# Gate and up products of two SwiGLUs by Strassen's scheme, down products as a second stage

## The chip, the cores and the metric

The kernel runs on one core of one Trainium2 chip. Its time is the device time of one execution in microseconds (us), the median of several runs. The core's engines run unsynchronized, each through its own queue in order: TensorE (PE in the profile, its weight loads PEld) multiplies matrices, VectorE (DVE) and ScalarE (ACT) do element-wise work and can read PE's accumulation banks in PSUM, GpSimd (POOL) does element-wise work on SBUF alone, and SyncE (SP) issues nearly all DMA transfers here. An instruction that waits holds up all that stands behind it on its engine.

## What is computed

One layer on x of 1024 tokens by 1024 features, float32, in three steps with a final norm. The token mixing between the two SwiGLUs is the same before and after.

```python
def rms_norm(x, g):
    y = x * lax.rsqrt(jnp.mean(x * x, axis=-1, keepdims=True) + NORM_EPS)
    return y * g
def swiglu(x, w_gate, w_up, w_down):       # w_gate, w_up: 1024 x 2816, w_down: 2816 x 1024
    return (jax.nn.silu(x @ w_gate) * (x @ w_up)) @ w_down

x = x + 0.5 * swiglu(rms_norm(x, ffn1_norm), ffn1_w_gate, ffn1_w_up, ffn1_w_down)
x = x + token_mixing(rms_norm(x, mix_norm))   # attention, mLSTM, output product
x = x + 0.5 * swiglu(rms_norm(x, ffn2_norm), ffn2_w_gate, ffn2_w_up, ffn2_w_down)
return rms_norm(x, final_norm)
```

## The kernel before

Everything lies transposed: features on the 128 partitions, tokens along the free axis, in two halves of 512 tokens (`HALVES`). A float32 product is made of three matmuls: each operand is split into a high part (ScalarE copies it to float32r) and a low part (the operand minus its high part, on VectorE), and `mm3` (L337) adds high x high, high x low and low x high in one PSUM bank. One matmul has 128 x 128 weights and 512 tokens.

`Weights` (L44) streams all weights of the program in one fixed order through three rings: a raw unit of 128 x 1024 (`wraw`, two buffers, loaded by SP), its high part (`whi`, four buffers, L71) and its low part (`wlo`, four, L83). A `get` splits the unit two places ahead, and loading runs ahead of splitting, over the borders between the stages of the program as well.

The order of all instructions is the program's own (`manual_schedule`). Side work is written as generators that stand in a list `bg`; `pump` (L264) lets each of them issue one more piece between two products, and `drain` issues the rest.

A SwiGLU is the function `ffn` (L343). The 22 blocks of 128 hidden features are taken in four groups of 6, 6, 5 and 5 (`GROUPS`). For each block, gate (w = 0) and up (w = 1) are multiplied for both halves of the tokens, 8 blocks of input features by 3 matmuls each; `evac` (L348) turns two such banks into a gated row, high and low part, in SBUF: a multiply by 1/rms (L351), tanh on ScalarE (L352), and so on to L358. After each group `down` (L414) multiplies its gated rows by the down weights for the 8 blocks of output features and adds the result to the rows of x in SBUF (L427). In the last group the first half goes through all output blocks ahead of the second, so that the next norm (`norm`, L312, with `rstd_of`, L280, for 1/rms) can begin.

The products start on rows that aren't normed yet: `gained` (L306) multiplies by the norm's gain and splits (L309, L310), and 1/rms of each token is applied to the product in `evac`. The first SwiGLU starts with `W.start`, which loads its first units in halves; `SHIFT` times `WARM` = 12 small matmuls on a constant matrix run while the first loads are on their way (L467). The second SwiGLU starts behind the output product of the second half (L1200 on), whose loop also prepares its rows; its first weight units are loaded and split meanwhile.

`late_consts` (L203) makes constants for the mixing within the first SwiGLU.

## Time and profile before

| | |
|---|---|
| median of 3 runs | 2546.78 us (2544.69 to 2547.41) |
| span of the profiled execution | 2542.7 us |
| PE busy | 2500.0 us, 98% |
| VectorE, ScalarE, GpSimd busy | 1268.5, 771.4, 251.5 us |
| DMA | 182 MB, 72 GB/s on average |

The profiled execution is one run of the program; its span reaches from the first to the last instruction. Busy times are sums over the span, and stages differ: GpSimd's, for instance, lie in the token mixing almost alone. An engine's idle time costs something only where another engine waits for it.

### The profile page before, as it was taken

How to read it: one execution, taken by the hardware profiler on the slowest of the kernel's cores; microseconds unless marked ns; L12 is line 12 of the kernel's file. 1: busy time of each engine (PE TensorE's matmuls, PEld its weight loads, DVE VectorE, ACT ScalarE, POOL GpSimd, SP SyncE). 2: the span in 40 equal slices, each digit the busy share in tenths (PEclk: the TensorE clock that was granted, in tenths of full speed). 3: DMA queues.
4: the chain of work that ended last, by engine and by line, in shares of the span. 5: the costliest groups of instructions: out<-in, count | busy, mean ns of one | idle time of the engine just before them, and what ended most of it. 6: DMA issues, size and time to landing. Idle time of an engine off the chain costs nothing.

```text
span 2542.7 us, 29518 instructions
## 1 busy us (share of the span) xinstructions
PE 2500.0 (98%) x11856; PEld 2077.6 (82%) x11856; DVE 1268.5 (50%) x2188; ACT 771.4 (30%) x1438; POOL 251.5 (10%) x218
## 2 busy tenths in 40 slices
PE   9999999999998999999999999999999999999997
PEld 7888888888887878888877788888888888888886
DVE  6533433434458873555658944545553343343444
ACT  5211111112236642333346623333321121111123
POOL 0000000000034330000234400000000000000003
PEclk9999999999999999999999999999999999999999
DMA  3111111121242212222532122224211111111113
GB/s 133 53 50 50 46 46 58 38 62 43 77 142 65 71 61 85 77 84 85 179 96 63 53 83 86 69 86 150 83 40 44 59 48 44 55 39 56 50 40 118
DMA packets 64841, 182.08 MB, mean 72 GB/s; under 512 B 7488, under 2 KB 12736, under 8 KB 64704
## 3 DMA queue, kind: packets, MB, share of 16 engines
q1 hardware_dynamic: 62640, 179.20, 22.4%
q8 instruction: 93, 1.52, 0.3%
q0 software_dynamic: 1200, 0.79, 0.2%
q14 instruction: 44, 0.36, 0.0%
q10 hardware_dynamic: 864, 0.21, 0.0%
HBM read 168.90 MB, written 11.27 MB: 71 GB/s over the span
## 4 chain that ended last, share of the span: by engine, by line
PE 86%; DVE 9%; ACT 2%; issue 1%; DMA 1%; SPq 0%; DVEq 0%; POOL 0%; ACTq 0%
PE mm L338 26%; PE mm L339 26%; PE mm L340 26%; DVE P L811 1%; PE mm L672 1%; DVE PT L850 1%; PE mm L673 1%; PE mm L674 1%; DVE P L831 1%; DVE wlo L83 1%; PE lm L952 1%; PE lm L980 1%; PE lm L975 1%; PE lm L978 1%; DVE s L621 0%
## 5 line engine op out<-in xcount | busy, mean ns | idle before, releaser
L338 PE MATMUL mm<-s,whi 128*128 128x512 f32 (+1 forms) x2992 | 1174.5, 393 | 1.9 <-ACT s L309 0.9
L340 PE MATMUL mm<-s,wlo 128*128 128x512 f32 (+1 forms) x2992 | 1165.4, 389 | 2.8 <-POOL wlo L83 2.8
L339 PE MATMUL mm<-s,whi 128*128 128x512 f32 (+1 forms) x2992 | 1164.6, 389 | 0.9 <-DVE s L310 0.9
L340 PEld LDWEIGHTS mm<-s,wlo 128*128 128x128 f32 x2992 | 563.5, 188 | 122.3 <-POOL wlo L83 4.9
L338 PEld LDWEIGHTS mm<-s,whi 128*128 128x128 f32 x2992 | 563.5, 188 | 118.5 <-issue 4.1
L339 PEld LDWEIGHTS mm<-s,whi 128*128 128x128 f32 x2992 | 564.1, 189 | 113.4 <-DVE s L310 2.2
L71 ACT ACTIVATE whi<-wraw 128x1024 fp32r<-128x1024 f32 (+3 forms) x320 | 310.8, 977 | 359.0 <-PE mm L339 269.3
L83 DVE TENSOR_TENSOR wlo<-wraw,whi 128x1024 fp32r<-128x1024 f32 (+2 forms) x290 | 333.6, 1151 | 100.0 <-ACT whi L71 99.0
L427 DVE SCALAR_TENSOR_TENSOR X<-mm,X 128x512 f32<-128x512 f32 (+1 forms) x132 | 88.5, 675 | 274.5 <-PE mm L340 274.4
L352 ACT ACTIVATE mm<-nsq 128x512 f32<-128x512 f32 x88 | 53.0, 602 | 380.3 <-DVE nsq L351 380.3
L351 DVE TENSOR_TENSOR nsq<-mm,nr 128x512 f32<-128x512 f32 x88 | 60.8, 691 | 213.8 <-PE mm L340 188.4
L355 DVE TENSOR_TENSOR nsq<-nsq,mm 128x512 f32<-128x512 f32 x88 | 60.4, 687 | 176.3 <-PE mm L340 176.1
L83 POOL TENSOR_TENSOR wlo<-wraw,whi 128x1024 fp32r<-128x1024 f32 (+1 forms) x30 | 61.2, 2043 | 702.9 <-ACT whi L71 701.3
L357 ACT ACTIVATE s<-nsq 128x512 fp32r<-128x512 f32 x64 | 40.5, 632 | 272.2 <-DVE nsq L356 268.4
L288 POOL TENSOR_TENSOR nv<-nv,mhalf 128x4 f32<-128x4 f32 (+1 forms) x9 | 11.2, 1242 | 911.4 <-DVE nv L287 911.4
L353 DVE SCALAR_TENSOR_TENSOR nsq<-mm,nsq 128x512 f32<-128x512 f32 x88 | 60.9, 692 | 58.9 <-ACT mm L352 58.9
L340 PE MATMUL mm<-gb,wlo 128*128 128x512 f32 (+1 forms) x196 | 75.5, 385 | 0.0
L339 PE MATMUL mm<-gb,whi 128*128 128x512 f32 (+1 forms) x196 | 75.5, 385 | 0.0
L338 PE MATMUL mm<-gb,whi 128*128 128x512 f32 (+1 forms) x196 | 75.5, 385 | 0.0
L672 PE MATMUL mm<-whi,s 128*128 128x256 f32 x256 | 74.1, 289 | 0.0
L673 PE MATMUL mm<-whi,s 128*128 128x256 f32 x256 | 72.5, 283 | 0.0
L674 PE MATMUL mm<-wlo,s 128*128 128x256 f32 x256 | 72.4, 283 | 0.0
(229 smaller groups left out, 2161.0 us busy)
## 6 DMA issues: line engine op xcount, KB each, us to landing
wraw<-gu SPq DMA_DIRECT2D x86, 512.0 KB, 3.7
wraw<-win SPq DMA_DIRECT2D x84, 512.0 KB, 3.5
wraw<-dn SPq DMA_DIRECT2D x48, 320.0 KB, 2.9
wraw<-dn SPq DMA_DIRECT2D x32, 384.0 KB, 3.1
wraw<-wmv SPq DMA_DIRECT2D x16, 512.0 KB, 3.2
wraw<-wpa SPq DMA_DIRECT2D x16, 512.0 KB, 3.2
wraw<-wpm SPq DMA_DIRECT2D x16, 512.0 KB, 3.2
wraw<-wwo SPq DMA_DIRECT2D x16, 512.0 KB, 3.3
```

Source lines behind the costliest of these rows:

```text
L71: self.nc.scalar.activation(hv, v, AF.Copy)
L83: (self.nc.gpsimd if self.on_pool else self.nc.vector).tensor_sub(lv, v, hv.bitcast(F32))
L338: nc.tensor.matmul(ps, hi, xh, start=first, stop=False)
L339: nc.tensor.matmul(ps, hi, xl, start=False, stop=False)
L340: nc.tensor.matmul(ps, lo, xh, start=False, stop=last)
L351: nc.vector.tensor_mul(t, ps, R[h])
L353: nc.vector.scalar_tensor_tensor(t, ps, 1.0, t, op0=OP.add, op1=OP.mult)
L355: nc.vector.tensor_mul(t, t, ps)
L427: nc.vector.scalar_tensor_tensor(x, ps[p], 0.25, x, op0=OP.mult, op1=OP.add)
L672: nc.tensor.matmul(ps, x[:, 0], hi, start=k == 0, stop=False)
L673: nc.tensor.matmul(ps, x[:, 1], hi, start=False, stop=False)
L674: nc.tensor.matmul(ps, x[:, 0], lo, start=False, stop=k == KT - 1)
```

## The change

Gate and up products are computed by the Winograd form of Strassen's scheme. The matrix of weights is cut into 2 x 2 blocks (two blocks of hidden features by two halves of the input features), the rows of x into 2 x 2 blocks as well (two halves of the features by two halves of the tokens); seven products of sums of blocks take the place of eight products. Since sums of x blocks mix tokens, the rows must be normed before: x times gain times 1/rms.

- `mixed` makes the sums of x blocks on GpSimd and splits them into high and low parts. Products 1 and 2 need only the first half of the tokens and no sums. They are done for two pairs of hidden blocks (s = 0 and 1) at the start, while `lead` norms the other half and runs `mixed`.
- `gate_up` goes through 11 pairs s of hidden blocks, with products in the order 1, 2, 6, 7, 4, 5, 3. Weight sums are made on GpSimd (`sums`, `last_sum`). A product's weights are split four products ahead (`split`, the same rings of four buffers). Products 1 and 2, then 6, 7 and 4, then 5 and 3 accumulate in one bank each; what is added from other banks is added by VectorE (`group`).
- `gated` writes the gated rows to a DRAM buffer `gd`. The down products follow as a second stage, in chunks of 2, 4, 4, 4, 4 and 4 hidden blocks: `fetch` loads a chunk's rows and splits them while the chunk before is multiplied; x is loaded again for the residual.
- Temporary rows of 128 x 512 share one ring of 24 buffers (`RING`).
- The second SwiGLU's weights don't belong to the stream of `Weights` any longer (`W.limit`); its first loads are issued when the output product is through. Its first half of rows is normed within the output product (`early`), with sums of squares on GpSimd.
- `W.start` is gone; the warm-up has 48 matmuls (`SHIFT` 12). `late_consts` runs at the end of `lead`. Final rows are stored one by one instead of in pairs.

```diff
-GROUPS = (6, 6, 5, 5)
+CHUNK = 4
+CHUNKS = [(0, FT % CHUNK)] + [(f, CHUNK) for f in range(FT % CHUNK, FT, CHUNK)]
+RING = 24
+PRODUCTS = (1, 2, 6, 7, 4, 5, 3)
-SHIFT = 3
+SHIFT = 12
...
+    def parted(x, hi, lo):
+        nc.scalar.activation(hi, x, AF.Copy)
+        nc.vector.tensor_sub(lo, x, hi.bitcast(F32))
+
+    def mixed(pool, Xn, op, own):
+        for k in range(4):
+            own[k] = [temp(pool, R32) for _ in range(2)]
+            t = temp(pool)
+            nc.gpsimd.tensor_sub(t, Xn[4 + k][1], Xn[k][1])
+            parted(Xn[4 + k][1], *own[k])
+            nc.gpsimd.tensor_sub(Xn[k][1], Xn[k][1], Xn[k][0])
+            nc.gpsimd.tensor_add(Xn[k][0], Xn[k][0], t)
+            nc.gpsimd.tensor_sub(Xn[4 + k][0], Xn[4 + k][0], Xn[k][0])
+            parted(Xn[k][0], op[6](k, 0), op[6](k, 1))
+            yield
+            parted(t, op[7](k, 0), op[7](k, 1))
+            parted(Xn[4 + k][0], op[4](k, 0), op[4](k, 1))
+            parted(Xn[k][1], op[5](k, 0), op[5](k, 1))
+            yield
...
+        def split(s, p):
+            if s == S2:
+                return
+            src = raw[s, *{1: (0, 0), 2: (0, 1), 6: "S2", 7: (0, 0), 4: (1, 1), 5: (1, 0), 3: (0, 1)}[p]]
+            hi = wpool.tile([128, UNIT], R32, name="whi", bufs=4)
+            lo = wpool.tile([128, UNIT], R32, name="wlo", bufs=4)
+            parted(src, hi, lo)
...
+        def sums(s):
+            if s < S2:
+                a11, a21, a22 = raw[s, 0, 0], raw[s, 1, 0], raw[s, 1, 1]
+                raw[s, "S", "2"] = t = pool.tile([128, UNIT], F32, name="wr", bufs=4)
+                nc.gpsimd.tensor_sub(a11, a11, a21)
+                nc.gpsimd.tensor_sub(t, a22, a11)
+                nc.gpsimd.tensor_add(a21, a21, a22)
+
+        def last_sum(s):
+            if s < S2:
+                nc.gpsimd.tensor_sub(raw[s, 0, 1], raw[s, 0, 1], raw[s, "S", "2"])
...
+        def gated(s, m, half, z, w, src):
+            if w == 0:
+                st["th"] = temp(pool)
+                nc.scalar.activation(st["th"], z[0], AF.Tanh, scale=0.5)
+            else:
+                th = st.pop("th")
+                nc.vector.scalar_tensor_tensor(th, th, 1.0, z[0], op0=OP.add, op1=OP.mult)
+                nc.vector.tensor_mul(th, th, z[1])
+                nc.sync.dma_start(gd[2 * s + m, :, half * HS:(half + 1) * HS], th)
+
+        def group(s, p):
+            for w in range(2):
+                ps = product(s, p, w, p in (1, 6, 5))
+                if p == 1:
+                    st[s, "s1", w] = t = temp(pool)
+                    nc.scalar.activation(t, ps, AF.Copy)
+                elif p == 2:
+                    st[s, "z", w] = ps
+                    gated(s, 0, 0, [st.get((s, "z", v)) for v in range(2)], w, p)
+                elif p in (6, 7):
+                    st[s, f"u{p}", w] = t = temp(pool)
+                    nc.vector.tensor_add(t, ps, st[s, "s1", w])
+                else:
+                    key, m, half = {4: ("s1", 1, 0), 5: ("u7", 1, 1), 3: ("u6", 0, 1)}[p]
+                    z = st[s, key, w]
+                    nc.vector.tensor_add(z, ps, z)
+                    gated(s, m, half, [st[s, key, v] for v in range(2)], w, p)
...
+        order = [(s, p) for s in range(2) for p in (1, 2)]
+        order += [(s, p) for s in range(S2) for p in PRODUCTS if s > 1 or p not in (1, 2)]
+        rest = iter(order[4:])
+        yield
+        sums(0)
+        last_sum(0)
+        for j, (s, p) in enumerate(order):
+            if j == 4:
+                for _ in lead:
+                    pass
+            group(s, p)
+            if j < 4:
+                next(lead, None)
+                next(lead, None)
+            nxt = next(rest, None)
+            if nxt:
+                split(*nxt)
...
+        def normed(h, r, ks=range(KT)):
             for k in ks:
+                nc.vector.scalar_tensor_tensor(X[k][h], X[k][h], gains[:, 0, k:k + 1], r, op0=OP.mult, op1=OP.mult)
+                if h == 0:
+                    o = op[1 + k // 4]
+                    parted(X[k][h], o(k % 4, 0), o(k % 4, 1))
                 yield
+
+        def lead():
+            acc = temp(pool)
             for k in range(KT):
+                stats(pool, acc, X[k][1], k == 0, nc.gpsimd)
+                if k % 4 == 3:
+                    yield
+            for r in rstd_of(pool, psum, [acc]):
+                yield
+            for _ in normed(1, r):
+                pass
+            yield
+            yield from mixed(pool, X, op, own)
+            late_consts(pool)
...
+    def early():
+        for k in range(KT):
+            stats(pool, acc[0], X[k][0], k == 0, nc.gpsimd)
+            if k % 2:
+                yield
+        for r in rstd_of(pool, psum, acc[:1]):
+            yield
+        for k in range(KT):
+            nc.vector.scalar_tensor_tensor(X[k][0], X[k][0], gains[:, 2, k:k + 1], r, op0=OP.mult, op1=OP.mult)
+            parted(X[k][0], t0[:, k, 0], t0[:, k, 1])
+            yield
```

## Rows read from the trace of the kernel before

**Rows 1.** The page: busy time, share and instructions of each engine.
```profile
PE 2500.0 (98%) x11856; PEld 2077.6 (82%) x11856; DVE 1268.5 (50%) x2188; ACT 771.4 (30%) x1438; POOL 251.5 (10%) x218
```
**Rows 2.** Windows: stretch, its length, engines' busy time (instructions), PE clock, DMA share, GB/s.
```profile
10.00:20.00 10.00, 9.23 (x40) 7.07 (x39) 9.26 (x14) 9.96 (x18) 0.00 (x0) 1.00 0.99 366
...
250.00:400.00 150.00, 150.00 (x663) 124.24 (x662) 56.15 (x73) 25.85 (x34) 0.00 (x0) 1.00 0.16 48
```
**Rows 3.** Timeline of PE at 600: start, length, operation; 21 matmuls lie between.
```profile
600.41 0.39 PE L338 MATMUL mm<-s,whi 128*128 128x512 f32 x1
...
605.17 0.39 PE L338 MATMUL mm<-s,whi 128*128 128x512 f32 x1
```
**Rows 4.** Groups by shape: line, engine, operation, count; busy us, mean ns; idle before.
```profile
L83 DVE TENSOR_TENSOR wlo<-wraw,whi 128x1024 fp32r<-128x1024 f32 x218 | 268.2, 1231 | 89.0 <-ACT whi L71 88.7
...
L358 DVE TENSOR_TENSOR s<-nsq,s 128x512 fp32r<-128x512 f32 x64 | 44.3, 693 | 46.3 <-ACT s L357 46.3
...
L71 ACT ACTIVATE whi<-wraw 128x1024 fp32r<-128x1024 f32 x234 | 244.9, 1051 | 201.4 <-PE mm L339 124.6 <-DMA wraw<-win 21.2 <-PE mm L673 16.5
...
L357 ACT ACTIVATE s<-nsq 128x512 fp32r<-128x512 f32 x64 | 40.5, 632 | 272.2 <-DVE nsq L356 268.4 <-PE mm L285 3.8
...
L83 POOL TENSOR_TENSOR wlo<-wraw,whi 128x1024 fp32r<-128x1024 f32 x16 | 38.3, 2396 | 48.9 <-ACT whi L71 47.2 <-PE mm L340 1.7
```
**Rows 5.** Line 330's own view: shortest, median and longest ns, first and last start.
```profile
L330 POOL TENSOR_TENSOR s<-nsq,s x16: 1272/1300/2062, 717.0 to 1263.7; 128x512 fp32r<-128x512 f32 x16
```
**Rows 6.** Timelines of POOL and DVE around 732 and around 838.
```profile
731.77 1.27 POOL L330 TENSOR_TENSOR s<-nsq,s 128x512 fp32r<-128x512 f32 x1
...
731.90 2.00 DVE L83 TENSOR_TENSOR wlo<-wraw,whi 128x816 fp32r<-128x816 f32 x1 [1.48 <-ACT whi L71]
...
734.43 0.99 DVE L83 TENSOR_TENSOR wlo<-wraw,whi 128x816 fp32r<-128x816 f32 x1
...
837.10 1.29 DVE L850 TENSOR_TENSOR PT<-pt,s 128x512 fp32r<-128x512 f32 x2
...
837.89 1.29 POOL L881 TENSOR_TENSOR s<-ot,s 64x512 fp32r<-64x512 f32 x1
```
**Rows 7.** Timeline of PE at the start; 51 matmuls lie before the last row.
```profile
1.50 4.21 PE L467 MATMUL mm<-ident 128*128 128x128 f32 x18 [1.50 <-DVE ident L198]
...
6.17 0.51 PE L338 MATMUL mm<-s,whi 128*128 128x512 f32 x1 [0.46 <-ACT s L309]
...
20.66 0.39 PE L338 MATMUL mm<-s,whi 128*128 128x512 f32 x1
```
**Rows 8.** Timeline of DVE at the end: the 1/rms chain's first step and its use.
```profile
2532.93 0.16 DVE L287 TENSOR_SCALAR nv<-mm 128x2 f32<-128x2 f32 x1 [1.11 <-PE mm L285]
...
2534.92 0.42 DVE L1230 TENSOR_TENSOR X<-X,nr 128x256 f32<-128x256 f32 x1 [1.16 <-ACT nr L295]
```
**Rows 9.** PE's timeline after an idle of 2.50 us, and the window behind it.
```profile
783.23 0.19 PE L755 MATMUL ag<-s,gselT 8*32 8x4 f32 x2 [2.50 <-DVE s L749]
...
784.00:787.20 3.20, 3.20 (x13) 2.77 (x12) 2.33 (x16) 1.46 (x4) 0.00 (x0) 0.51 0.54 164
```
**Rows 10.** Timelines of PE and SP where the second output product begins.
```profile
1758.38 0.47 PE L338 MATMUL mm<-s,whi 128*128 128x512 f32 x1 [0.87 <-DVE s L1137]
...
1759.05 0.33 SPq L1188 DMA_DIRECT2D X<-xd  x1
```
**Rows 11.** DMA issues: queue, count, KB each, median us from issue to landing.
```profile
wraw<-gu SPq DMA_DIRECT2D x86, 512.0 KB, 3.7
...
X<-xd SPq DMA_DIRECT2D x16, 256.0 KB, 5.4
```
**Rows 12.** Timeline of DVE: first and last of the constants' operations, 19 in all.
```profile
65.62 0.19 DVE L221 TENSOR_SCALAR bhalf<-binf 128x42 f32<-128x42 f32 x1 [0.30 <-DMA binf<-binf]
...
69.31 0.17 DVE L249 COPY gselT<-ident 128x32 f32<-128x32 f32 x1
```
**Rows 13.** Waits of PE between 700 and 760: us in total, times, longest.
```profile
PE mm L648 <- DVE wlo L83: 1.5, 1, 1.5
```

More of the change, by code (lines that the diff above doesn't have):

```diff
@@ L51, in __init__ @@
         self.on_pool = False
+        self.limit = None
     def load_to(self, n):
-        while self.loaded < min(n, len(self.plan)):
+        n = min(n, len(self.plan) if self.limit is None else self.limit)
+        while self.loaded < n:
             key, src = self.plan[self.loaded]
@@ L181, in layer @@
     plan_mix()
+    W.limit = len(W.plan)
     plan_ffn(2)
@@ L255, in nbufs, with temp @@
     def nbufs(p):
-        return 2 if p in two else 4
+        return RING if p in wide else 2 if p in two else 4
+    def temp(p, dt=F32):
+        return p.tile([128, HS], dt, name="nsq", bufs=nbufs(p))
     two = []
@@ L452, in ffn @@
-            gs0 += G
+                    pump()
+                for q in QUARTERS if quarter else ():
+                    for d, unit in quarter.items():
+                        down(c, d, q, unit)
+                        done(d, q)
+                        pump()
+                        pump()
+    gd = dram.tile([FT, 128, S], F32, name="gd")
     with ExitStack() as c1:
@@ L497, in layer @@
+        next(f1)
+        for k in range(KT):
+            loadx(k, 1)
+        acc = temp(pool)
+        for k in range(KT):
+            stats(pool, acc, X[k][0], k == 0)
+        for r in rstd_of(pool, psum, [acc]):
+            pass
+        for _ in normed(0, r):
+            pass
+        next(f1)
         Hm = []
@@ L1210, in layer, with operand, lead2 @@
                 W.mid()
-        x = X[:, d, HS:]
+            if k in (2, 5):
+                pump()
+        x = X[d][1]
         nc.vector.scalar_tensor_tensor(x, ps, 0.5, x, op0=OP.mult, op1=OP.add)
-        ready(0, d)
-        ready(1, d)
-    for h in range(2):
-        bg.append(rstd_task(pool, psum, acc[h], R, 1 + 4 * h))
+        nc.sync.dma_start(xd[1, :, d], x)
+        stats(pool, acc[1], x, d == 0)
+        pump()
+    drain()
+    t = [t0, slot(1, [KT, 2, HS]), slot(2, [KT, 2, HS])]
+    own = {}
+    def operand(p):
+        if p == 3:
+            return lambda k, i: own[k][i]
+        i, k0 = {1: (0, 0), 2: (0, 4), 6: (1, 0), 7: (1, 4), 4: (2, 0), 5: (2, 4)}[p]
+        return lambda k, x: t[i][:, k0 + k, x]
+    op = {p: operand(p) for p in PRODUCTS}
+    def lead2():
+        for r in rstd_of(pool, psum, acc[1:]):
+            yield
+        for k in range(KT):
+            nc.vector.scalar_tensor_tensor(X[k][1], X[k][1], gains[:, 2, k:k + 1], r, op0=OP.mult, op1=OP.mult)
+        yield
+        yield from mixed(pool, X, op, own)
     fa = {}
```

359 lines of the change are left out of this document (177 added, 182 removed).

## The prediction, made before the result was known

> **What bounds the kernel now.** I read the page's busy times first, then the windows of one stretch of the first SwiGLU, then PE's timeline there. PE is busy for 98% of the span [rows 1]; in a steady stretch it never rests and has the full clock, while VectorE works 56 us of 150 and GpSimd nothing [rows 2]. A 128x512 matmul follows the last one after 4.76 us / 21 = 0.2267 us [rows 3]. So a matmul taken away is worth 0.2267 us, and every wait that PE is given costs its whole length. The other engines have room on average; what must be asked is which waits they put before PE.
>
> **What is removed.** A SwiGLU's gate and up products are 22 x 2 x 2 x 8 x 3 = 2112 matmuls; in seven products of eight they are 11 x 7 x 24 = 1848. 264 fewer in each SwiGLU, 528 x 0.2267 = 119.7 us. The down products keep their 1056. One product for gate and up (a "group", 24 matmuls) lasts 5.44 us, one pair of f blocks (seven groups) 38.1.
>
> **What GpSimd and VectorE do to each other.** The change gives GpSimd 16 sums of 128x512 (`mixed`) and 4 of 128x1024 for each pair of f blocks (`sums`, `last_sum`). Alone, such an operation takes 1.30 and 2.40 us [rows 4, 5]. Beside VectorE it is another matter: at 731.77 a GpSimd subtraction ran until 733.04, and the low part of 128x816 that VectorE began at 731.90 took 2.00 us where the same shape takes 0.99; it ended 0.86 after GpSimd did. An operation that reads PSUM went on undisturbed (two L850 in 1.29 us, beside a GpSimd operation of 1.29) [rows 6]. I read: a VectorE operation with two SBUF inputs (every low part is one) and a GpSimd sum take turns. The Trainium skill says it as a rule (SBUF — State Buffer, section "Who interferes with whom"): the pair of ports is locked for a whole instruction by whichever starts first, and VectorE with at most one SBUF input is spared. Row and rule agree, and the rule speaks against this change; what the sum is without turns is worked out as a rival below.
>
> **Entry of the first SwiGLU.** Before, 51 matmuls were done by 20.66 [rows 7], as if PE had started at 9.1 and never waited. Now the rows must be normed first.
> 1. The warm-up is 48 matmuls instead of 12. The 12 lasted from 1.5 to 5.7; the rest at up to twice the pace puts the end at 12 to 18 us. x (2 MB of the first 3 MB) is there by about 10 at 366 GB/s [rows 2], its squares are summed by 11.5. The 1/rms chain took 2.0 us for two blocks from its first VectorE step to its use [rows 8]; with four blocks and the matmuls ahead 3.5: it ends at 16 (up to 22).
> 2. Eight rows, each a multiply 0.7, a high part 0.63, a low part 0.69 [rows 4]. They alternate between two in-order engines, so a row costs 2.1 us: 33. The weight parts stand behind them in both queues: high 1.05, low 1.23; the third matmul needs the low part at 34.6. PE has been idle, and after 2.5 us of idling the granted clock was 0.51 (the 1.2 GHz level) for 3.2 us [rows 9], which costs 1.6 us. Groups 1 and 2 end at 41.3 and 46.7.
> 3. GpSimd meanwhile does four weight sums in turns with three low parts (9.6 + 3.7, from 34.6 to 47.9), and only then, in order, seven sums of squares in turns with a low part (9.1 + 1.2, to 58.3). The matmul on them stands in PE's queue ahead of group 3: PE waits 11.6 us, and the clock costs 1.6 again. Group 3 ends at 65.9, behind it the transposes; 1/rms at 67.2, the fifth normed row at 70.5, and `mixed` begins.
> 4. `mixed` up to the operand that ends group 5's first half: 16 sums (20.8) in turns with 17 low parts (11.7), three multiplies (2.0) and a weight's low part (1.2): 35.7, so 106.2, and the last three matmuls to 106.9. Without waits 4.5 groups would have ended at 9.1 + 24.5 = 33.6. **Loss 73.3.**
>
> **Entry of the second SwiGLU.** In the output product PE now has the first half's 1/rms matmuls behind 42 matmuls (1758.38 + 9.5 = 1767.9). GpSimd's seven sums start about 5 us after the loads at 1759.05 [rows 10, 11] and take 9.1 + 2.2 in turns: 1775.6. PE waits 7.7, the clock costs 1.6: 9.3. The weight loads now wait, on SP's queue, for the store of the last row: with 0 at the last output matmul, VectorE and SP's issue 1.35, landing 3.7 [rows 11], high 1.05, low 1.23: 7.4 for the third matmul. Before, they were loaded ahead. Clock 1.6; group 1 ends at 14.0. GpSimd's weight sums begin when the fifth load is there and the low parts are done (11.6), and end at 22.4; the power at 23.7; PE waits for it before group 3. 1/rms at 25.1, `mixed` from 28.5, with 20.8 + 11.7, three weight parts 3.7, multiplies 2.0 and group 4's evacuation 1.4: 68.1, plus 0.7, against 24.5 without waits. **Loss 44.3.**
>
> **Behind the entries.** In the first SwiGLU the constants (3.9 us of VectorE, 65.62 to 69.48 [rows 12], behind a small load) now stand ahead of the first additions, which PE needs: 3. The sums of the second pair come late behind `mixed`: 3 in each. **9**, between 0 and 20.
>
> **Steady state.** Per pair VectorE has 7 x 1.23 + 18 x 0.69 = 21 us of work, GpSimd 9.6, ScalarE 11, of 38.1: no engine is full, and DMA (3 MB per 38 us) is far from 366 GB/s. But the turns come at one place. With 0 at the end of product 2 (they run in the order 1, 2, 6, 7, 4, 5, 3), GpSimd's sums for the next pair start behind a low part at 13.3 and last three times 2.40. Product 4 ends at 16.3; its VectorE queue is an addition to 17.0, then a gating step that waits for GpSimd until 18.05 (ends 18.6), the next until 20.95 (21.5), a low part (22.65), and only then product 5's first addition, to 23.3. Product 3 accumulates in the bank that this addition reads, and would start at 21.76. PE waits 1.6 us, in nine pairs of each SwiGLU: **29** (0 if the turns fall otherwise, 58 if each such wait costs the clock too).
>
> **Other edges.** The norm ahead of the mixing has 8 x 0.68 us less cover (12 matmuls for a down product, not 15), and PE already waited 1.5 there [rows 13]: 3, between 0 and 6. While the first, half-size chunk runs (21.7 us) 7 MB of x, gated rows and weights arrive, 19 us at 366 GB/s: 2, between 0 and 10. The high and low parts of the fetched rows (30 us of each engine spread over 239 us), more residual additions (96 for 64), the stores of gated rows, and the final stores by one row lie beside PE's work: nothing, at worst 2 at the tail.
>
> **The sum.** 73.3 + 44.3 + 9.3 + 9 + 29 + 5 = 169.9 against 119.7: 50 us slower than the profiled span of 2542.7, so 2592.7; the median of the runs lies 4.1 above that span, so 2597.
>
> **Rivals.**
> *No turns.* If GpSimd and VectorE run side by side, the weight sums end 3.7 earlier, `mixed` is GpSimd's chain alone (20 us to the needed operand), nothing stalls in the steady state: entries 53.5 and 23.7, the early wait 7.8, behind them 3, other edges 5: 93 against 119.7, 2520. It decides from the point where the low parts stop lengthening. Against it: [rows 6]. For it: with engines this empty the turns may fall into slack.
> *Turns in the entries alone.* The steady order may put the gating step ahead of GpSimd: 2597 - 29 = 2568.
> *The clock.* If each steady wait is followed by a stretch at the 1.2 GHz level, 18 x 1.6 more: 2626. For it: one idle of 2.5 us did it [rows 9]; against it: each wait of 1.6 us is shorter than that. The Trainium skill (TensorE: Matmul & The Clock Gate, "HAM oscillation — how this bites in real kernels") tells of a kernel in which every tile's wait starts the next tile cold; no row here shows that.
> *The scheme does not do what it says*, for example that matmuls into a bank already in use come slower: then the pitch is above 0.2267 and the time far above; nothing in the trace speaks for it.
>
> **Chances and range.** Forecast (2575 to 2615) 0.33; turns in the entries alone 0.27; clock 0.14; no turns 0.18; in between, near no change, 0.08. A measurement can tell 0.2% (5 us) from nothing. Faster 0.19, same 0.06, slower 0.75. The range takes in half of "no turns" and nearly all of "clock": 2518 to 2632.
>
> **What would show it.** The pitch of 0.2267 unchanged and 528 matmuls fewer; PE's first product near 34 us; an idle stretch of some 11 us near 50 and a stuttering one from 70 to 105; a gap of 7 us behind the output product and stuttering for 30; VectorE's low parts above 0.69 and 1.23 where GpSimd runs; in each pair a wait of PE for an addition, at product 3. I am wrong if `mixed` lasts 21 us, not 35, or if the steady stretch has no waits.

## The result, and the profile after

The changed kernel takes 2609.59 us (median of 4 runs, 2608.09 to 2613.49); the kernel before, beside it, 2545.81. The ratio is 1.0252, 95% interval 1.0238 to 1.0267: slower by 63.8 us. The profiled span is 2606.9 us, 64.2 above before's 2542.7. The forecast was 2597, the range 2518 to 2632.

First the page of after: engines' busy time with share and instructions, then PE's busy tenths and the granted clock in 40 slices.

```profile
PE 2427.5 (93%) x11370; PEld 2001.1 (77%) x11370; DVE 1544.5 (59%) x2386; ACT 874.2 (34%) x1546; POOL 537.6 (21%) x344
...
PE   5599999999999999999999999998869999999997
...
PEclk7799999999999999999999999998879999999998
```

PE has less to do, and is busy for 93% instead of 98% [rows 1]. The lost time stands where it was forecast, at the two entries and in the output product ahead of the second: the first two slices and slices 28 to 30. (An entry is the stretch from a SwiGLU's first products to the point from which they follow each other; a group is one product for gate and up.) PE's timeline shows that a matmul costs what it cost before; of these two rows the second is 21 matmuls later, (322.76 - 318.00) / 21 = 0.2267 us [rows 3].

```profile
318.00 0.39 PE L394 MATMUL mm<-nsq,wlo 128*128 128x512 f32 x1
...
322.76 0.39 PE L394 MATMUL mm<-s,wlo 128*128 128x512 f32 x1
```

So 528 x 0.2267 = 119.7 us were gained, and 119.7 + 64.2 = 183.9 were lost. The waits of PE over the whole run (what waited, for what: us in total, times, longest) name most of it; the last row shown is the final norm's sum over its squares, at 2587.6:

```profile
PE mm L394 <- DVE s L330: 35.3, 7, 10.0
PE mm L394 <- DVE nsq L424: 26.2, 18, 1.5
PE mm L394 <- ACT whi L329: 24.1, 2, 17.4
PE mm L263 <- POOL nsq L256: 20.7, 2, 10.8
PE mm L394 <- ACT s L329: 13.4, 4, 4.6
...
PE mm L310 <- DVE nsq L528: 7.3, 3, 2.6
...
PE mm L263 <- DVE nsq L256: 5.3, 1, 5.3
```

By stage (from the span's start to the first matmul of the token mixing; to the last matmul on the mixing's state; to the last matmul of the down products; to the end of the span):

| | before | after | difference |
|---|---|---|---|
| first SwiGLU | 731.9 | 767.6 | +35.7 |
| token mixing (code unchanged) | 971.4 | 976.4 | +5.0 |
| output product and second SwiGLU | 827.4 | 850.9 | +23.5 |
| behind the last down product | 12.0 | 12.0 | 0 |

The windows of after give the clock (columns as in [rows 2]): the entry of the first SwiGLU, a steady stretch, the output product, the entry of the second.

```profile
35.00:110.00 75.00, 37.18 (x124) 27.34 (x123) 50.05 (x53) 23.52 (x39) 49.79 (x30) 0.68 0.12 38
...
250.00:400.00 150.00, 144.17 (x633) 118.21 (x632) 93.00 (x96) 39.78 (x47) 40.02 (x16) 1.00 0.24 79
1799.00:1862.00 63.00, 50.72 (x204) 40.38 (x204) 29.92 (x40) 21.01 (x31) 10.77 (x8) 0.86 0.40 136
...
1868.00:1926.00 58.00, 33.22 (x120) 24.48 (x121) 47.83 (x40) 22.44 (x35) 42.30 (x22) 0.74 0.23 80
```

The steady wait is best seen in one pair, on the timelines of POOL, DVE and PE (start, length, operation, idle before and what ended it):

```profile
308.44 2.40 POOL L379 TENSOR_TENSOR wr<-wr,wraw 128x1024 f32<-128x1024 f32 x1
310.80 2.86 POOL L380 TENSOR_TENSOR wr<-wr 128x1024 f32<-128x1024 f32 x1
...
309.23 0.69 DVE L424 TENSOR_TENSOR nsq<-mm,nsq 128x512 f32<-128x512 f32 x1 [2.03 <-PE mm L394]
309.84 1.56 DVE L405 SCALAR_TENSOR_TENSOR nsq<-nsq 128x512 f32<-128x512 f32 x1
311.44 2.77 DVE L406 TENSOR_TENSOR nsq<-nsq 128x512 f32<-128x512 f32 x1
314.13 1.21 DVE L330 TENSOR_TENSOR wlo<-wr,whi 128x1024 fp32r<-128x1024 f32 x1
315.26 1.28 DVE L424 TENSOR_TENSOR nsq<-mm,nsq 128x512 f32<-128x512 f32 x2
...
316.09 0.70 PE L394 MATMUL mm<-nsq,whi 128*128 128x512 f32 x2 [1.46 <-DVE nsq L424]
```

GpSimd's weight sums stretch product 4's gating steps (the two operations L405 and L406 of `gated`) from 0.69 to 1.56 and 2.77. A low part stands behind them, so product 5's first addition comes only at 315.26. Product 3 accumulates in the bank that this addition reads, and waits 1.46 us. The clock is 1.00 before and behind it.

The rows also show what a turn is. L405 ends at 311.40, 0.56 behind the end of the sum L379 (310.84), and L406 at 314.21, 0.55 behind L380 (313.66); alone such a step takes 0.69. L380 in its turn ends 2.26 behind L405, and takes 2.40 alone. So each engine waits for nearly all of the other's operation, but 0.13 to 0.14 of either overlaps. Product 4's second addition, with one of its operands in PSUM, is not stretched: 0.69 at 309.23, beside L379.

### The profile page after: what moved, and what is told of

The parts are those of the page before. It is cut to its first block, busy times and chain, and to the rows that moved or that the text cites. A ratio compares the mean times of both kernels' runs of the same rounds, so it can differ in the third digit from the quotient of the medians.

```text
span 2606.9 us, 29897 instructions
## 1 busy us (share of the span) xinstructions
PE 2427.5 (93%) x11370; PEld 2001.1 (77%) x11370; DVE 1544.5 (59%) x2386; ACT 874.2 (34%) x1546; POOL 537.6 (21%) x344
## 4 chain that ended last, share of the span: by engine, by line
PE 75%; DVE 15%; issue 4%; ACT 3%; DMA 2%; POOL 1%; SPq 0%; DVEq 0%; POOLq 0%; ACTq 0%
PE mm L394 27%; PE mm L310 13%; PE mm L312 13%; PE mm L311 13%; DVE wlo L330 1%; DVE P L936 1%; PE mm L797 1%; DVE s L330 1%; DVE PT L975 1%; PE mm L798 1%; PE mm L799 1%; DVE nsq L405 1%; DVE wlo L88 1%; DVE nsq L424 1%; DMA nsq<-gd 1%
## 5 line engine op out<-in xcount | busy, mean ns | idle before, releaser
L394 PE MATMUL mm<-s,whi 128*128 128x512 f32 x2112 | 666.6, 396 | 72.9 <-DVE s L330 35.3
L310 PE MATMUL mm<-s,whi 128*128 128x512 f32 (+1 forms) x1776 | 705.2, 397 | 10.5 <-DVE nsq L528 7.3
L312 PE MATMUL mm<-s,wlo 128*128 128x512 f32 (+1 forms) x1776 | 695.2, 391 | 2.1 <-POOL wlo L88 1.4
L311 PE MATMUL mm<-s,whi 128*128 128x512 f32 (+1 forms) x1776 | 694.0, 391 | 0.0
L394 PE MATMUL mm<-s,wlo 128*128 128x512 f32 x1056 | 417.5, 395 | 0.1
L76 ACT ACTIVATE whi<-wraw 128x1024 fp32r<-128x1024 f32 (+2 forms) x210 | 215.1, 1028 | 146.6 <-PE mm L311 46.5
L528 DVE SCALAR_TENSOR_TENSOR nsq<-mm,nsq 128x512 f32<-128x512 f32 (+1 forms) x196 | 132.0, 679 | 177.5 <-PE mm L312 155.8
L394 PEld LDWEIGHTS mm<-s,wlo 128*128 128x128 f32 x1056 | 201.9, 191 | 43.5 <-DVE wlo L330 1.5
L330 DVE TENSOR_TENSOR wlo<-wr,whi 128x1024 fp32r<-128x1024 f32 x110 | 141.1, 1283 | 96.2 <-ACT whi L329 92.4
L329 ACT ACTIVATE whi<-wr 128x1024 fp32r<-128x1024 f32 x110 | 116.2, 1057 | 181.0 <-PE mm L394 177.7
L330 DVE TENSOR_TENSOR s<-nsq,s 128x512 fp32r<-128x512 f32 x136 | 112.9, 844 | 61.7 <-ACT s L329 61.7
L424 DVE TENSOR_TENSOR nsq<-mm,nsq 128x512 f32<-128x512 f32 x132 | 89.2, 686 | 87.9 <-PE mm L394 87.1
L394 PE MATMUL mm<-nsq,whi 128*128 128x512 f32 x352 | 110.1, 394 | 26.2 <-DVE nsq L424 26.2
L420 DVE TENSOR_TENSOR nsq<-mm,nsq 128x512 f32<-128x512 f32 x88 | 60.8, 691 | 108.4 <-PE mm L394 108.4
```

The costliest lines, as they stand in the source:

```text
L76: self.nc.scalar.activation(hv, v, AF.Copy)
L310: nc.tensor.matmul(ps, hi, xh, start=first, stop=False)
L311: nc.tensor.matmul(ps, hi, xl, start=False, stop=False)
L312: nc.tensor.matmul(ps, lo, xh, start=False, stop=last)
L329: nc.scalar.activation(hi, x, AF.Copy)
L330: nc.vector.tensor_sub(lo, x, hi.bitcast(F32))
```

## The experiments

All times are medians in us, the ratio is to the kernel before on the same chip. "First stage" and "last stages" are the first and third row of the table above, from each kernel's profile.

| kernel | time | ratio, 95% | first stage | mixing | last stages |
|---|---|---|---|---|---|
| changed kernel | 2609.59 | 1.0238 to 1.0267 | 767.6 | 976.4 | 850.9 |
| e1_wsums | 2596.64 | 1.0181 to 1.0212 | 760.8 | 975.2 | 843.9 |
| e2_mixed | 2599.88 | 1.0188 to 1.0222 | 763.1 | 978.7 | 844.8 |
| e3_squares | 2599.69 | 1.0196 to 1.0226 | 761.9 | 976.6 | 847.5 |
| e4_order | 2602.78 | 1.0205 to 1.0235 | 762.2 | 976.3 | 850.4 |
| e5_place | 2575.59 | 1.0103 to 1.0137 | 752.2 | 973.9 | 835.7 |
| n1_entry | 2549.53 | 1.0004 to 1.0028 | 740.6 | 975.7 | 817.5 |
| n2_gpsums | 2533.12 | 0.9937 to 0.9967 | 728.3 | 975.6 | 809.9 |
| n3_gpmix | 2553.35 | 1.0020 to 1.0043 | 740.3 | 975.3 | 823.4 |
| n4_spread | 2509.04 | 0.9837 to 0.9870 | 719.0 | 976.4 | 800.5 |
| n5_tight | 2494.52 | 0.9784 to 0.9813 | 709.0 | 974.1 | 792.5 |
| n6_gpmix | 2503.18 | 0.9816 to 0.9845 | 716.0 | 976.0 | 796.3 |
| n7_warm3 | 2493.63 | 0.9778 to 0.9811 | 712.8 | 973.0 | 792.8 |

The theory was that of the prediction: GpSimd's sums and VectorE's operations take turns, and this is what PE waits for. The rival was that the place in an in-order queue decides: what stands ahead of the operation that PE needs next, turns or not.

**Steady waits, e1_wsums and e5_place.** The first takes GpSimd out, the second leaves it in and moves the work.

```diff
 def sums(s):                      # e1_wsums, and likewise last_sum
-    nc.gpsimd.tensor_sub(a11, a11, a21)
+    eng = nc.gpsimd if s < 2 else nc.vector
+    eng.tensor_sub(a11, a11, a21)
...
```

> From the third pair on, the four weight sums of each pair run on VectorE instead of GpSimd (nothing else moves; the first two pairs keep them on GpSimd). Turns: in the changed kernel PE waits 18 times, 26.2 us in all, for product 5's first addition, which stands behind two gating steps that take 1.32 and 1.34 us on the average instead of 0.69. Without GpSimd's sums those steps fall to 0.69, the 18 waits go, and VectorE, which gets 4 x 1.23 = 4.9 us more work per pair, is still early enough (product 4's additions end by 17.7, both gating steps by 19, the low part by 20.2, product 5's first addition by 20.9, and product 3 starts at 21.8): 2609.6 - 26 = 2583 (2579 to 2588). Rival, VectorE's order alone: the addition is late because of what is queued ahead of it, turns or not; then 4.9 us more in the same queue leave the waits or lengthen them: 2609 to 2640. Rival, the clock: if each wait also costs a slow stretch, the gain is well above 26, down to 2555.

Measured: 13 us less, half of the 26, between what theory and rival said. The 18 waits are all there, at 0.77 us each. VectorE's timeline, then PE's row among the waits:

```profile
302.87 1.23 DVE L379 TENSOR_TENSOR wraw<-wraw,wr 128x1024 f32<-128x1024 f32 x1
304.13 1.22 DVE L380 TENSOR_TENSOR wr<-wr,wraw 128x1024 f32<-128x1024 f32 x1
305.27 1.22 DVE L381 TENSOR_TENSOR wr<-wr 128x1024 f32<-128x1024 f32 x1
306.40 1.28 DVE L426 TENSOR_TENSOR nsq<-mm,nsq 128x512 f32<-128x512 f32 x2
...
PE mm L396 <- DVE nsq L426: 13.9, 18, 0.8
```

No turn is taken now (the gating steps last 0.69), but the three sums stand in VectorE's queue ahead of product 4's additions, the fourth (at 310.38) stands directly ahead of product 5's first addition, and the delay reaches that addition all the same.

```diff
-    nxt = next(rest, None)                                   # e5_place
+    nxt = order[j + 4] if j + 4 < P else order[j + 3] if j + 3 >= P else None   # P: pair 2, product 1
     if nxt:
+        if nxt[0] > 1 and nxt[1] == 6:
+            sums(nxt[0])
         split(*nxt)
...
-    if p == 1:
-        sums(s)
```

> The changed kernel with one thing moved, from the third pair on: a pair's three weight sums, still on GpSimd, start behind product 3 of the pair before instead of behind product 7, the fourth one product later, and weights are split three products ahead instead of four. Entries, output product and amounts of work stay. Place theory: GpSimd's sums now run beside products 1 and 2, behind which no product waits for VectorE; VectorE's operations still get longer beside them, but the 18 waits at product 3 (26.2 us) go: 2583 (2579 to 2588). Rival (turns cost wherever they fall): waits of the same size come at another product, 2600 to 2610. Rival (the sums come so late that product 6 waits for its weights): new waits before product 6, 2595 or above.

Measured: 34 us less than the changed kernel, and not one wait for product 5's addition is left in the whole run. The groups of VectorE from 250 to 400 in e5_place (line, operation, shapes, count, busy us, mean ns) and the window:

```profile
L405 DVE SCALAR_TENSOR_TENSOR nsq<-nsq 128x512 f32<-128x512 f32 x12 | 20.3, 1694 | 0.4
L406 DVE TENSOR_TENSOR nsq<-nsq 128x512 f32<-128x512 f32 x12 | 16.6, 1384 | 0.4
...
250.00:400.00 150.00, 150.00 (x664) 124.20 (x663) 98.64 (x98) 40.73 (x51) 40.03 (x16) 1.00 0.25 83
```

The turns are as costly as before (1694 and 1384 ns on the mean, where the changed kernel has 1401 and 1447), GpSimd does the same sums, and PE is busy for 150.00 of 150. Only the place is another. It is not the place that the expectation named, which was right about the waits and wrong about where the sums run: GpSimd's queue holds nothing but these sums, so they start as soon as the low part of product 1's weight is taken, which now is one product later; they run beside product 5's gating steps, and late additions behind product 3 hold nobody up. 26.2 of the 34 are the waits; the mixing took 2.5 less, and some 4 in the two SwiGLU stages are not accounted for.

**The entries, one suspect at a time: e2_mixed, e3_squares, e4_order.**

```diff
 def mixed(pool, Xn, op, own):     # e2_mixed: all four sums
-        nc.gpsimd.tensor_sub(t, Xn[4 + k][1], Xn[k][1])
+        nc.vector.tensor_sub(t, Xn[4 + k][1], Xn[k][1])
...
-        stats(pool, acc, X[k][1], k == 0, nc.gpsimd)        # e3_squares, and in early()
+        stats(pool, acc, X[k][1], k == 0)
...
+        split(0, 1), split(0, 2)                            # e4_order: ahead of the rows
...
+        # row k + 1 is multiplied before row k's low part is taken
```

> The sixteen sums of `mixed` run on VectorE instead of GpSimd, in both SwiGLUs; everything else stays. Turns: a sum on GpSimd holds VectorE up for nearly its whole length, so GpSimd and VectorE together are one queue: from 71.0 to 105.4 in the first SwiGLU. On VectorE alone it is 16 sums x 0.69 + 17 low parts x 0.69 + a weight's low part 1.23 + what stands between, 25 to 27 instead of 34: 9 less in the first entry and 8 to 9 in the second: 2592 (2587 to 2598). Rival, no turns: the two engines work side by side and the stage is as long as GpSimd's chain of 16 x 1.6 = 26 us and its edges; with all on VectorE nothing gets shorter, 2609 to 2620.

> The seven additions of squares that GpSimd does in each SwiGLU's entry (second half of the tokens in the first, first half in the second) run on VectorE. PE's two longest single waits, 10.8 us at 56 (behind GpSimd's four weight sums) and 9.9 at 1819 (in the output product), are for these additions. If they are what bounds those places, both go, with the slow clock behind them: 10.8 + 9.9 + 2 to 4 for the clock less what VectorE's in-order queue gives back (seven additions of 0.69 among the low parts): 2588 (2582 to 2595). Rival: the entry is bounded by what comes after (weight sums on GpSimd ahead of `mixed`, and the low parts), so that only the output product gains: 2598 to 2602. Rival: VectorE gets the additions behind low parts that wait for late weights, and nothing is won: 2605 or above.

> First SwiGLU's entry in another order: the first pair's two weight units are split while the first 1/rms is on its way (ahead of the normed rows instead of behind them), and the rows are staggered (VectorE multiplies row k+1 before it takes row k's low part). Engines and amounts of work stay, GpSimd included. Theory (in-order queues): PE's first product comes at 17 to 19 instead of 31.9; a row takes 1.4 us, or up to 1.7 where GpSimd's weight sums, which now start near 20, take turns with it; GpSimd's squares end 10 to 12 earlier, so all that follows is as much earlier: 2598 (2594 to 2604). Rival (the entry is bounded by the total of what VectorE and GpSimd must do in turns, in any order): the gain in the first product is given back by 105, 2605 to 2610.

Measured: 9.7, 9.9 and 6.8 us less, each about half of what was expected. In e2_mixed the sums and low parts last from 75.43 to 101.7 on VectorE, 26 us as expected, but begin 4.4 us later than on GpSimd (71.05), since VectorE first has the rest of the multiplies, a weight's low part and two gating steps in its queue. The time of e3_squares lies in the range of its first rival, but not for that rival's reason: the first stage gave 5.7 us, the last stages 3.4. In e3_squares the additions stand behind ScalarE's squares and still run beside GpSimd's weight sums; PE's wait falls from 10.82 to 5.40, and in the output product from 9.89 to 7.5 only. In e4_order PE starts 11.2 us earlier and then waits longer. The rows, from PE's timelines of e3_squares and of e4_order:

```profile
51.73 1.84 PE L263 MATMUL mm<-mean,nsq 128*128 128x2 f32 x8 [5.40 <-DVE nsq L256]
```

```profile
20.69 1.52 PE L394 MATMUL mm<-s,whi 128*128 128x512 f32 x2 [5.35 <-ACT s L594]
...
51.90 1.87 PE L263 MATMUL mm<-mean,nsq 128*128 128x2 f32 x8 [12.52 <-POOL nsq L256]
...
99.85 0.79 PE L394 MATMUL mm<-s,whi 128*128 128x512 f32 x1 [4.59 <-DVE s L330]
```

The last wait of the entry ends at 99.85, 5.5 earlier than in the changed kernel (105.35). So each suspect carries a part, and behind each one the next is already waiting. How large each part is, these runs don't say, since they were made one at a time from a kernel in which the others remain.

**All at once: n1_entry, n2_gpsums, n3_gpmix.** The products, and the number of sums and low parts, stay; the entry is written out by hand.

```diff
-        yield from mixed(pool, X, op, own)                  # n1_entry: product 6's operand first
+    def row(k, r, prev):
+        # two multiplies, two sums, product 6's high part; then the low part of row k - 1
...
+    both(0, 6); split(0, 7); ...; both(0, 7); raw4(k), raw5(k); ...   # other operands, a product ahead of PE
...
-    sums(0)                       # on GpSimd, ahead of all
+    sum1(0), sum2(0), split(0, 6) # on VectorE, each where its product is next
...
+    next(f2)                      # second SwiGLU: loads and first splits inside the output product
...
-                SUM.tensor_sub(...)                                   # n2_gpsums, from n1_entry, and the three others
+                (nc.vector if s < 2 else nc.gpsimd).tensor_sub(...)
...
-        MIX = nc.vector                                               # n3_gpmix, from n1_entry: the sums of rows
+        MIX = nc.gpsimd
```

> All the suspects put right at once, with the same seven products and the same matmuls. All sums of rows, squares and weights leave GpSimd. Entry of the first SwiGLU: the first pair's weights are split behind the second normed row, rows are staggered, the squares of the second half are summed by PE (eight accumulating matmuls for each block of tokens), the operand of the third product (6) is made first for all rows and the other operands after it, one product ahead of PE, the products of the first pair run row by row. Entry of the second: weights loaded and split during the output product, the rest as in the first. Steady: a pair's three weight sums stand behind product 3 of the pair before, where no product waits for VectorE, the fourth one product later, weights are split three products ahead instead of four. Theory (what costs is work that stands in an in-order queue ahead of what PE needs next, with turns making it longer): first product near 18, product 6 from 50 on, the first pair done by 90 instead of 135: 40 to 45 gained; second entry 30 to 35; output product 10 to 15; 26 for the 18 waits: 2490 (2480 to 2515), 55 below the kernel before. Rival (the entries are bounded by VectorE's total work, some 75 us of low parts, sums and additions from the first row to the last operand, in any order): gains of 15 in each entry at most, 2530 to 2545.

> As n1_entry, but from the third pair on the four weight sums of a pair run on GpSimd again, at the new place (behind product 3 of the pair before). Place theory (a turn costs only where a product of PE waits for VectorE next): no wait at product 3 comes back, same as n1_entry within 4 us. Rival (turns with GpSimd cost wherever they fall): some of the 26 us come back, 8 to 26 above n1_entry.

> As n1_entry, but the sixteen sums of rows in each entry run on GpSimd. Turns: a pair of a GpSimd sum and a VectorE low part or multiply takes 1.67 us where VectorE alone does both in 1.38, and a sum that nothing runs beside takes 1.3 to 1.6 instead of 0.69, so each entry gets 8 to 12 longer: 16 to 24 above n1_entry. Rival (no turns: GpSimd takes 11 us of work off VectorE in each entry): 5 to 15 below n1_entry.

Measured: n1_entry gains 60 us and ends 0.2% above before's time, 60 short of what was expected and above its rival's range; n2_gpsums, with the steady sums back on GpSimd, is 16 faster than n1_entry and below before. Neither its theory nor its rival had that: for steady work VectorE is the worse place for these sums. In n1_entry a new wait of PE comes 19 times, 16.3 us. One of them, 3.3, lies in the first entry, where n2_gpsums has it too (1.7); the other 18, 0.72 each and 13.0 in all, lie in the steady stretches, and n2_gpsums has none of them. The timelines of VectorE, ScalarE and PE in n1_entry:

```profile
262.41 1.22 DVE L365 TENSOR_TENSOR wr<-wr,wraw 128x1024 f32<-128x1024 f32 x1
...
263.75 1.06 ACT L329 ACTIVATE whi<-wr 128x1024 fp32r<-128x1024 f32 x1 [5.55 <-DVE wr L365]
264.71 1.07 ACT L404 ACTIVATE nsq<-mm 128x512 f32<-128x512 f32 x2
...
265.34 0.73 PE L383 MATMUL mm<-s,whi 128*128 128x512 f32 x2 [0.72 <-ACT nsq L404]
```

ScalarE's high part waits for the sum at the end of VectorE's queue, product 1's copy out of PSUM stands behind it on ScalarE, and product 2 waits for the copy. n3_gpmix differs from n1_entry by 4 us only, between its theory and its rival: its first stage is as long (740.3 against 740.6), its last stages 5.9 longer.

What else n1_entry and n2_gpsums lose is on PE's timelines. Of n2_gpsums:

```profile
35.72 9.63 PE L263 MATMUL mm<-mean,s 128*128 128x2 f32 x64
...
114.61 1.19 PE L383 MATMUL mm<-s,whi 128*128 128x512 f32 x2 [8.02 <-DVE nsq L410]
...
1775.62 1.84 PE L263 MATMUL mm<-mean,nsq 128*128 128x2 f32 x8 [6.79 <-DVE nsq L256]
```

PE's own sum of the squares takes 9.63 us, where seven additions on VectorE would be 5 (an estimate, 7 x 0.69); the gating steps of the first pair, put off to one heap, hold up pair 2 by 8.0 us in both SwiGLUs; the 1/rms matmul in the output product stands ahead of its data.

**The version that beats both: n4_spread, n5_tight.**

```diff
+    for k in range(1, KT):                                  # n4_spread: squares on VectorE again
+        nc.vector.tensor_add(sq1(0), sq1(0), sq1(k))
...
+    gate(); split(0, 7); ...; gate(); raw4(k)               # gating steps spread
-    for k in range(4): raw5(k)                              # ahead of product 7's additions
+    evac(0, 7, 0, ...), evac(0, 7, 1, ...)
...
+        for _ in range(4): yield                            # early(): 1/rms four steps later
...
-    sum3(0); split(0, 5); low(5, 0) ... low(5, 3)           # n5_tight
+    sum3(0); low(5, 0), low(5, 1); split(0, 5); low(5, 2), low(5, 3)
```

> From n2_gpsums, whose entries still lose time at four places: PE's own sum of squares (9.6 us, VectorE idle for 9.3 of them, 1/rms at 51 instead of 42), gating steps of the first pair put off to one heap (12 VectorE operations ahead of the first addition of pair 2: PE waits 8.0, in both SwiGLUs), the additions of product 7 behind eight row sums (PE waits 2.2 and 3.8 before product 4), and the 1/rms matmul of the output product ahead of its data (PE waits 6.8). Here the squares are added on VectorE behind the rows, the gating steps are spread, the additions of product 7 come ahead of the sums for product 5, the matmul of the output product stands four steps later, and the second SwiGLU's weights are loaded over five steps of the output product. In-order theory: 9 + 2 x 8 + 2 + 3 + 7 and the clock behind some of them: 35 to 40 below n2_gpsums, 2495 (2485 to 2510). Rival (VectorE's total work bounds the entries; a wait taken away at one place comes back at the next): 10 to 15 below n2_gpsums, 2518 to 2523.

> n4_spread with four operations of the entries in another place: the low part of a weight sum no longer stands directly behind its sum in VectorE's queue (VectorE was idle four times for 1.2 us there, for ScalarE's high part), product 5's additions stand ahead of two of the low parts that product 3 needs last, the last gating step of the first pair stands behind the additions of product 7, and the first weight's high part stands ahead of the first row's. Theory (VectorE's queue is what bounds an entry from the first row to 110): 4 to 5 less idle of VectorE, 2 to 3 less wait at product 3 and 2 at product 4 in each entry: 6 to 12 below n4_spread, 2500 (2496 to 2504). Rival (PE is bounded by the data chain, not by the order of VectorE's queue): same as n4_spread, 2506 to 2512.

Measured: 24.1 less, then 14.5 less, both beyond what the rivals allow; the first is short of the 35 to 40, the second above the 6 to 12. n5_tight is 2.0% faster than the kernel before (0.9784 to 0.9813) and 4.4% faster than the changed kernel, with the same 528 matmuls removed. The page of its profile, and its windows in the entry of the first SwiGLU and in the steady stretch:

```profile
PE 2407.3 (97%) x11370; PEld 1989.8 (80%) x11370; DVE 1564.3 (63%) x2448; ACT 864.0 (35%) x1546; POOL 421.9 (17%) x282
...
44.00:60.00 16.00, 10.76 (x44) 7.61 (x42) 15.60 (x24) 7.36 (x12) 0.00 (x0) 1.00 0.04 16
60.00:89.00 29.00, 24.79 (x96) 18.86 (x96) 28.11 (x40) 10.90 (x18) 0.00 (x0) 0.94 0.25 82
...
250.00:400.00 150.00, 150.00 (x664) 124.20 (x663) 100.12 (x100) 41.24 (x52) 40.05 (x16) 1.00 0.25 81
```

From 44 to 89 VectorE is busy for 43.7 of 45 us (the sum of the two windows): in this stretch the entry is close to what VectorE's amount of work allows. In the changed kernel VectorE was busy for 50 of the 75 us from 35 to 110.

**The price of turns where VectorE is the bound, and the warm-up: n6_gpmix, n7_warm3.**

```diff
-    MIX = nc.vector               # n6_gpmix, from n5_tight
+    MIX = nc.gpsimd
...
-SHIFT = 12                        # n7_warm3, from n5_tight
+SHIFT = 3
```

> n5_tight with the sixteen sums of rows of each entry on GpSimd. In n3_gpmix the same step moved the time by 4 us, but there PE's own sum of squares and heaped gating steps stood in the way; in n5_tight VectorE is busy for 64 of the 69 us from 44 to 113. Turns price an entry whose bound is VectorE: sums of 1.49 to 1.63 us, multiplies of 1.26 instead of 0.75, low parts of 1.16 instead of 0.69 (as in n3_gpmix) against 11 us taken off VectorE: 4 to 9 longer in each entry, 2502 to 2512. Rival (no price in turns once the order is right): 2488 to 2498.

> n5_tight with 12 warm-up matmuls instead of 48, as before the change. The warm-up ends at 11.7 and the first 1/rms matmul stands behind it, PE then waits 1.35 and 2.15, and the clock in 15:25 is 0.66 all the same. Theory (the long warm-up neither costs nor gives): same as n5_tight within 3 us, 2491 to 2498. Rival (it keeps the clock up for the first products): 3 to 6 longer. Rival (it holds up the first 1/rms): 1 to 3 shorter.

Measured: n6_gpmix 8.7 us longer than n5_tight (7.3 when each is set against the kernel before on its own chip), at the low end of the turns' price, some 4 for an entry on average. That is a net price: the sums took 11 us of work off VectorE in each entry. The multiplies of rows, from 44 to 89, in n6_gpmix and then in n5_tight:

```profile
L447 DVE SCALAR_TENSOR_TENSOR nsq<-nsq,gains 128x512 f32<-128x512 f32 x7 | 9.0, 1331 | 0.0
...
L447 DVE SCALAR_TENSOR_TENSOR nsq<-nsq,gains 128x512 f32<-128x512 f32 x7 | 5.0, 745 | 0.0
```

n7_warm3 takes the same time as n5_tight. In its profile PE starts 1.6 us later (18.27), and from 15 to 25 the clock is 0.50 instead of 0.66, which the expectation had not allowed for. Its first stage is 3.8 longer and the whole span 2.9, but the profiled run of n5_tight is the fastest of its four (2489.4 us), 5 below their median. So the warm-up's worth is below what these runs can tell.

## Why the prediction was right, and where it was not

The direction was right, and the time lies within the range, by steps of which most held. 169.9 us of losses were forecast, 183.9 came. That the two are so close is partly luck: the terms below are off by up to 9 us, some up and some down. As measured they add up to 72.8 + 40.2 + 18.7 + 5.0 + 26.2 + 13.5 + 3.9 + 2.9 = 183.2.

1. *The gain.* 119.7 us, pitch 0.2267: held.
2. *Turns.* The two engines do hold each other up where both read two operands from SBUF. The Trainium skill's rule (SBUF — State Buffer, "Who interferes with whom") that VectorE with at most one SBUF input is spared agrees with the trace: product 4's second addition, which reads one operand from PSUM, takes 0.69 beside L379, where the gating steps behind it, which read SBUF alone, take 1.56 and 2.77. The size was off: a pair was put at 1.30 + 0.69 = 1.99 [rows 4, 5]. In `mixed` GpSimd's sums follow each other every 1.67 us (72.76, 74.43) with a VectorE operation beside each. The overlap was there to be read in [rows 6]: the low part ended 0.86 behind GpSimd, and takes 0.99 alone, so 0.13 of it had overlapped. With 0.14 off either operation a pair is 1.71, an estimate from the steady rows above.
3. *Entry of the first SwiGLU*, forecast 73.3. The steps and their rows of after's PE and POOL timelines:

```profile
1.50 10.20 PE L577 MATMUL mm<-ident 128*128 128x128 f32 x72 [1.50 <-DVE ident L173]
...
31.93 1.22 PE L394 MATMUL mm<-s,whi 128*128 128x512 f32 x2 [17.43 <-ACT whi L329]
56.16 1.87 PE L263 MATMUL mm<-mean,nsq 128*128 128x2 f32 x8 [10.82 <-POOL nsq L256]
...
105.35 0.79 PE L394 MATMUL mm<-s,whi 128*128 128x512 f32 x1 [4.59 <-DVE s L330]
...
71.05 1.63 POOL L337 TENSOR_TENSOR nsq<-nsq 128x512 f32<-128x512 f32 x1 [10.81 <-DVE nsq L587]
```

   The warm-up ended at 11.7 (12 to 18), the wait for GpSimd's squares was 10.82 (11.6), `mixed` began at 71.05 (70.5), the last operand came for 105.35 and the group's second half began at 106.4 (106.9). Loss 72.8. `mixed` came out right by errors that cancel: a pair took less than the 1.99, and against that stood a second weight's low part (at 85.05) and two gating steps (at 77.02 and 78.22), which the sum had left out.
4. *Entry of the second*, forecast 44.3: PE idle 6.68 behind the output product (7); the last wait of the stutter ends at 1925.38, 64.0 behind its end (68.1), so some 40.2.
5. *Behind the entries*, forecast 9: no wait of PE comes from the constants or from the second pair's sums. What comes is the clock: 0.89 from 106 to 130 and 0.93 from 1926 to 1960, 2.6 and 2.4 us, together 5.0.
6. *Steady state*, forecast 18 x 1.6 = 29: 18 waits, 26.2 us, at the product and for the addition named.
7. *The output product* was the term that was most off: forecast 9.3, measured 18.7 (from 1799.16 to 1861.39, 62.2 us for 192 matmuls, 43.5 at full clock). The wait for GpSimd's squares was 9.89 (7.7):

```profile
1818.85 1.87 PE L263 MATMUL mm<-mean,nsq 128*128 128x2 f32 x8 [9.89 <-POOL nsq L256]
```

   Two waits for late weights, of 1.1 and 0.5, had not been seen. PE is busy for 50.72 us in that window, 7.2 more than 43.5: 2.1 of these are the 1/rms matmuls themselves (1818.85 to 1820.58, 1826.06 to 1826.42), for which the sum had no term, and 5.1 are slower matmuls at a mean clock of 0.86, where 1.6 had been put.
8. *Other edges*, forecast 5, between 0 and 18. At the first chunk of the down products PE waits 4.7 us in the first SwiGLU and 3.7 in the second, in pieces of at most 2.6, and the clock behind them, 0.97 over 55 us, costs some 1.5 each: 11.4 instead of 2. The norm ahead of the mixing: 2.1 instead of 3 (below). Together 13.5. At the end PE waits 5.3 us for the squares (L263 in the list of waits), where it waited 1.4 for them before: 3.9, and the clock behind that; the tail had been put at nothing, at worst 2.
9. *The mixing* was not forecast to change beyond that; it took 5.0 longer. 2.1 come in its first 16 us. The windows of after:

```profile
770.60:773.60 3.00, 1.60 (x10) 1.38 (x11) 2.91 (x3) 0.60 (x2) 2.58 (x5) 0.98 0.18 14
773.60:776.60 3.00, 3.00 (x15) 3.00 (x14) 0.09 (x1) 0.00 (x0) 0.00 (x0) 0.50 0.84 269
```

   Before, one wait of 1.52 [rows 13], and the clock stayed at 1.00. After, two waits of 0.65 and 1.29 close together, and the clock falls to the 1.2 GHz level. But the same two waits stand there in e5_place, where the clock stays up:

```profile
755.20:758.20 3.00, 1.64 (x11) 1.43 (x12) 2.95 (x3) 0.56 (x2) 2.54 (x5) 1.00 0.27 16
758.20:761.20 3.00, 3.00 (x27) 3.00 (x26) 0.49 (x2) 0.00 (x0) 0.00 (x0) 1.00 0.79 262
```

   Twelve of the thirteen kernels with the scheme have these two waits. In the profiles of eight the clock falls behind them, in four (e1_wsums, e5_place, n3_gpmix, n5_tight) it does not, so the two waits alone don't decide it. Over the whole mixing the granted clock stands at 0.50 in five stretches of some 3 us before and in seven after. The thirteen kernels have five to eight of them, and the mixing takes 973.9 and 974.1 us in two with five (e5_place, n5_tight), 978.7 in the one with eight (e2_mixed). So part of the other 2.9 is this clock, which differs between profiles. Waits for ScalarE at line 893 are 1.9 (before 0.2). The rest is not settled.

By rivals: *the clock* was refuted in the form stated: after a steady wait of 1.46 the clock is 1.00. The Trainium skill's account (TensorE: Matmul & The Clock Gate, "HAM oscillation — how this bites in real kernels") of each wait starting the next tile cold is not what this steady stretch does; the waits of its example are longer. But the clock fell at the edges, where waits are longer or come in twos. *No turns* gave 2520 for a world without them; n5_tight, another order of the same scheme, went below that with the turns of GpSimd's steady sums still there.

The reason given, that turns cost the time, was half right. They make the steady wait, but their place makes it cost: e1_wsums took the turns away, put the sums into VectorE's queue and left half of the wait; e5_place left the turns and took all of it. In the entries the sums of rows on GpSimd cost some 4 us each, net, once the rest is in order (n6_gpmix against n5_tight); n6_gpmix, with these sums and the steady weight sums on GpSimd, is 106 us faster than the changed kernel. What cost the rest is the order: weight sums and squares on GpSimd ahead of the rows, rows that alternate between two engines, and operands made four at a time when PE needs one. The squares were moved alone (e3_squares), the rows were staggered together with earlier weight splits (e4_order), and each gave a part; the entry's weight sums and the order of the operands were changed only together with others (n1_entry), so their shares are argued and not measured.

## What to carry to other kernels

Before work is moved to an idle engine, ask what stands behind it in that engine's queue and which product waits for that: here the same weight sums cost PE 26 us of waits or none on GpSimd, and 14 or 13 on VectorE, by where they stood in the queue. A scheme with fewer products but with sums ahead of the first one pays its price at the entry; make the operand of the next product first for all rows, not all operands for one row. When one suspect explains a wait, change it alone and look at what waits next: three single changes gave 7 to 10 us each, the whole order 115.

## What was not expected of the hardware

Two short waits of PE close together (0.65 and 1.29 us) were followed by a clock of 0.50 for some 3 us in eight profiles and not in four others; single ones of 1.52 [rows 13] and of 1.46 were not followed by it in the rows shown. What decides it, no run here shows. PE's sum of eight squares for four blocks of tokens, 32 matmuls of two columns, took 9.63 us in n2_gpsums (64 records, 0.15 each; part of them at a clock of 0.50), 8.88 and 10.53 in n3_gpmix and n1_entry. Turns between GpSimd and VectorE are not quite whole: an operation that waited its turn ended 0.55 us behind the other where it takes 0.69 alone, and a pair took 1.67 us, less than the 1.99 that the rows of before add up to.
